# A hybrid DeltaNet / gMLP step: four weight pieces requested ahead of the second half of the modulation weights, and the halo rows in a tile of their own

## The chip, the cores and the metric

The kernel runs on one core of one Trainium2 chip. A core has five engines with a queue of instructions each: TensorE (PE, with the weight loads PEld), VectorE (DVE), ScalarE (ACT), GpSimd (POOL) and SyncE (SP), which here issues the DMA requests. The metric is the device time of one execution in microseconds. Before the change it was 2678.39 us, the median of three runs (2676.00 to 2682.14).

## The reference

One inference step of a layer over 128 context tokens and 2048 latent tokens, width 1024. Cut to what matters here:

```python
def modulation(cond, w_mod_l, b_mod_l):
    m = jax.nn.silu(cond) @ w_mod_l + b_mod_l
    return jnp.split(m[:, None, :], N_MOD, axis=-1)        # sh1, sc1, ga1, sh2, sc2, ga2

def mixer(h, s0, n_chunks, w_in_l, conv_l, ...):
    proj = h @ w_in_l
    qkv, gate, ab, u, vg = jnp.split(proj, cuts, axis=-1)
    qkv = jax.nn.silu(centred_conv(qkv, conv_l))           # width 3 over the tokens
    ...                                                    # bidirectional gated DeltaNet | gMLP
    return out @ w_out_l, s_new

def block(x, s0, mod, n_chunks, norm_mix_l, w_in_l, ...):
    sh1, sc1, ga1, sh2, sc2, ga2 = mod
    h = rmsnorm(x, norm_mix_l) * (1.0 + sc1) + sh1
    o, s_new = mixer(h, s0, n_chunks, w_in_l, ...)
    x = x + ga1 * o
    h = rmsnorm(x, norm_ffn_l) * (1.0 + sc2) + sh2
    x = x + ga2 * (jnp.square(jax.nn.relu(h @ w_ff1_l)) @ w_ff2_l)
    return x, s_new
```

`block` runs once for the context (modulated by the constant `c_ctx`) and once for the latent tokens (modulated by `c`). So the first projection `h @ w_in` needs the shift `sh1` and the scale `sc1` first, and those need `silu(cond) @ w_mod`.

## The kernel before

The 2176 tokens are 17 tiles of 128 rows. They are worked on in six blocks, five of three tiles and one of two. The kernel has three phases: the first projection with the convolution, the DeltaNet scan together with the gMLP and the output projection, and the feed-forward layer. The change lies at the start of the first phase.

Products of float32 are made in split form: an operand is cast to float32r on ScalarE (high part, `split_w`, line 194), and VectorE subtracts that from the original (low part, line 195). `mm3` (lines 220 to 222) then makes three matmuls of it: high by high, low by high, high by low.

At the start the shift and scale of the first norm are made by columns. The width of 1024 is eight column tiles of 128, and the vectors are made in halves of four column tiles. `mod_load(half, c0)` requests eight pieces of 128x512 of `w_mod`. `mod_columns` (from line 320) multiplies them with the two conditioning vectors in plain float32 (line 324), copies the resulting two rows on ScalarE (line 326), transposes them into columns (line 329) and adds the bias on VectorE (line 332); for the scale it adds one and multiplies by the norm's weight (line 336). There are four such calls: m0 gives the first half of the shift (`b1`), m1 the first half of the scale (`a1`), m2 and m3 the second halves of both.

The first block's rows (three tiles `x`, 512 KB each) are normalized by rows (`norm_rows`, line 301). The convolution looks one token to each side, so ten halo rows (`xh`) at the edges of the blocks are normalized, transposed and modulated apart (`hal`, `halH`, `halL`, `first_half`). Up to now `xh` takes one of the three buffers of the tag `x`, so that the third of the three row tiles waits until the halo rows have been transposed.

`column(k)` makes the operand of column tile k: three transposes on TensorE (line 471), scale and shift on ScalarE (`full`, line 473), then high and low part on VectorE (`kH`, line 476, and `kL`, line 477), plus single halo columns copied on GpSimd (lines 466 and 467). Columns 0 to 3 need the first halves of `a1` and `b1`, columns 4 to 7 the second halves. `feature_tile` then accumulates the eight columns against the pieces `W1` of `w_in`. The first three feature tiles of the first block are started by hand: columns 0 to 3 with their matmuls stand in the program ahead of `mod_columns(m2, ...)` and `mod_columns(m3, ...)`.

`make_masks` (from line 123) makes triangular masks for the scan: a memset on VectorE, twelve selects on GpSimd (lines 132 and 134), and differences on VectorE (lines 138 to 140).

The order on each engine is not the order of the program text. A planner goes through the instructions with its own estimate of the time and fixes, before anything runs, a sequence for each engine; on the chip each engine then keeps that sequence and waits on semaphores. SyncE issues the DMA requests in its sequence, with eight requests under way at a time: each waits for the landing of the one eight places ahead of it. Memory of a closed pool is used again by the pools of the next phase, whose first tiles wait for the last use of what lay there.

Of the kernel before, what the change touches and what calls it, by code (L numbers as in the profile page):

```python
# [8 lines left out]
F32 = mybir.dt.float32  # L9
# [8 lines left out]
P = 128  # L18
D = 1024
# [42 lines left out]
def hybrid_step(  # L62
# [118 lines left out]
    def raw_w(src, pool=None, tag="w"):  # L181
        t = (pool or wp).tile([P, 512], F32, tag=tag, name="raw")
        load(out=t, in_=src)
        return t
# [85 lines left out]
    with ExitStack() as ph:  # L270
        p1 = ph.enter_context(tc.tile_pool(name="p1", bufs=2, reuse_waits="tile"))
        pf = ph.enter_context(tc.tile_pool(name="p1f", bufs=2, reuse_waits="tile"))
# [43 lines left out]
        def mod_load(half, c0):  # L316
            return [raw_w(w_mod[0, k * P : (k + 1) * P, c0 + half * 512 : c0 + half * 512 + 512])
                    for k in range(KT)]

        def mod_columns(raws, half, dst, bias, scaled):  # L320

            pm = pm1()
            for k in range(KT):
                T.matmul(pm[0:2, :], scond[:, k, :], raws[k], start=k == 0, stop=k == KT - 1)
            row = p1.tile([2, 512], F32, tag="mrow", name="mrow", bufs=1)
            A.copy(row, pm[0:2, :])
            pc = pm1()
            for i in range(4):
                T.transpose(pc[:, 2 * i : 2 * i + 2], row[:, i * P : (i + 1) * P], ident[0:2, 0:2])
            ks = slice(half * 4, half * 4 + 4)  # L330
            d = dst[:, :, ks]
            V.tensor_tensor(out=d, in0=pc[:, 0:8].rearrange("p (k c) -> p c k", c=2),
                            in1=bias[:, ks].unsqueeze(1).to_broadcast([P, 2, 4]), op=ALU.add)
            if scaled:
                for cd in range(2):
                    V.scalar_tensor_tensor(out=dst[:, cd, ks], in0=dst[:, cd, ks], scalar=1.0,
                                           in1=vec[:, 16 + half * 4 : 20 + half * 4], op0=ALU.add, op1=ALU.mult)
# [25 lines left out]
        mod_columns(m0, 0, b1, vec[:, 0:8], False)  # L363


        xh = p1.tile([P, D], F32, tag="x", name="xh", bufs=3)[0:10, :]
        for m in range(5):
            r0 = 255 + 384 * m
            load(out=xh[2 * m : 2 * m + 2, :], in_=x_sample[0, r0 : r0 + 2, :])
# [9 lines left out]
        for t in BLOCKS[0]:  # L379
            x = p1.tile([P, D], F32, tag="x", name="x", bufs=3)  # L380
# [5 lines left out]
        def load_w1(gi, ks):  # L386
            return [w1_raw(gi, k) for k in ks]

        def w1_raw(gi, k):
            return raw_w(w_in[0, k * P : (k + 1) * P, gi * 512 : (gi + 1) * 512])  # L390
# [327 lines left out]
        blk, xs_, cols = prep_block(0)  # L718
        for st in xs_:
            st()  # L720
        m2 = mod_load(1, 0)
        m3 = mod_load(1, D)
        wr = load_w1(1, range(4))
        mod_columns(m1, 0, a1, vec[:, 8:16], True)
        W1[1] += [split_w(r) for r in wr]
        first_half(0)
# [3 lines left out]
        wr = load_w1(0, range(KT))  # L730
# [1202 lines left out]
```

## Time and profile before

| | us |
|---|---|
| median of three runs | 2678.39 (2676.00 to 2682.14) |
| the profiled execution: its time | 2678.03 |
| its span, first to last instruction | 2676.3 |
| TensorE busy | 2622.4 (98%) |
| VectorE busy | 1792.8 (67%) |
| ScalarE busy | 1245.4 (47%) |
| mean granted TensorE clock | 0.995 |

A row of a timeline gives the start, the duration, the engine, the line of the kernel, the operation, what it writes and reads, how many instructions are merged into the row, and in brackets the time that the engine stood idle before it and what ended that. A row of a view by stretches gives a stretch of time and the busy time of each engine in it, then the granted clock of TensorE (1.00 is full speed), the share of DMA that was busy, and GB/s. A matmul's duration is that of its passage through the array; back to back they start closer together than they last. A plain float32 matmul leaves two records.

### The profile page before, as it was taken

To read this page: it belongs to the slowest core of one execution; us is meant where nothing else is said; L and a number is where in the kernel's file an instruction comes from. 1 tells how busy PE (TensorE), PEld (TensorE's weight loads), DVE (VectorE), ACT (ScalarE), POOL (GpSimd) and SP (SyncE) were. 2 spreads that over 40 slices of the span, in tenths; PEclk is the share of its full clock that TensorE was granted. 3 is DMA by queue.
4 is the path that set the end of the run, shared out by engine and by line. 5 is a ranking of instruction groups with operands and counts; after the bars stand their busy time and mean duration, and the time that the engine had idled before them with its cause. 6 is when DMAs were issued, how large, how long until landed. Compare 5 with 4: busy or idle time off the path is not lost.

```text
span 2676.3 us, 45017 instructions
## 1 busy us (share of the span) xinstructions
PE 2622.4 (98%) x15698; PEld 2187.8 (82%) x15698; DVE 1792.8 (67%) x3694; ACT 1245.4 (47%) x3092; POOL 224.8 (8%) x448
## 2 busy tenths in 40 slices
PE   8999999999999999999999999999999999999998
PEld 5999998788887777788888888888888787888887
DVE  5867656766666778875688885566565556774874
ACT  4655555555554657763355543333242432332441
POOL 3111112111111111110000000000000000000000
PEclk9999999999999999999999999999999999999999
DMA  8867539655454657985868887443369978776772
GB/s 298 278 207 222 187 109 284 193 165 158 155 163 147 209 181 253 288 283 181 291 201 240 247 300 223 114 122 104 106 190 372 326 268 307 268 251 210 235 259 88
DMA packets 569385, 580.89 MB, mean 217 GB/s; under 512 B 35692, under 2 KB 401692, under 8 KB 565574
## 3 DMA queue, kind: packets, MB, share of 16 engines
q1 hardware_dynamic: 569158, 578.03, 67.6%
q8 instruction: 123, 2.02, 0.3%
q14 instruction: 104, 0.85, 0.1%
HBM read 398.14 MB, written 179.74 MB: 216 GB/s over the span
## 4 chain that ended last, share of the span: by engine, by line
PE 86%; DMA 6%; DVE 5%; ACT 1%; issue 1%; SPq 1%; POOL 0%; DVEq 0%; POOLq 0%; ACTq 0%
PE f L222 17%; PE f L220 17%; PE f L221 17%; PE pj L220 6%; PE pj L222 6%; PE pj L221 6%; PE pd L966 3%; PE pm L220 1%; PE pm L221 1%; PE pm L222 1%; PE pt L578 1%; PE pd L1140 1%; PE pd L1139 1%; DMA hop_d<-opL 1%; DMA qT<-qT_d 1%
## 5 line engine op out<-in xcount | busy, mean ns | idle before, releaser
L220 PE MATMUL f<-hop,zH 128*128 128x512 f32 x960 | 376.5, 393 | 1.2 <-ACT zH L1449 1.2
L221 PE MATMUL f<-hop,zH 128*128 128x512 f32 x960 | 377.1, 393 | 0.0
L222 PE MATMUL f<-hop,zL 128*128 128x512 f32 x960 | 376.9, 393 | 0.0
L220 PE MATMUL f<-hop,wH 128*128 128x512 f32 x896 | 354.0, 396 | 0.0
L221 PE MATMUL f<-hop,wH 128*128 128x512 f32 x896 | 350.7, 391 | 0.0
L222 PE MATMUL f<-hop,wL 128*128 128x512 f32 x896 | 350.6, 392 | 0.0
L1449 ACT CAST zH<-zraw 128x512 fp32r<-128x512 f32 x240 | 146.9, 621 | 297.1 <-DVE zraw L1443 86.4
L220 PEld LDWEIGHTS f<-hop,zH 128*128 128x128 f32 x960 | 180.4, 188 | 43.7 <-ACT zH L1449 1.6
L222 PEld LDWEIGHTS f<-hop,zL 128*128 128x128 f32 x960 | 180.3, 188 | 42.0 <-issue 0.9
L221 PEld LDWEIGHTS f<-hop,zH 128*128 128x128 f32 x960 | 180.1, 188 | 41.8 <-issue 0.9
L1443 DVE TENSOR_TENSOR zL<-zraw,zH 128x512 fp32r<-128x512 f32 x240 | 162.7, 687 | 66.4 <-ACT zH L1449 52.6
L222 PEld LDWEIGHTS f<-hop,wL 128*128 128x128 f32 x896 | 168.2, 188 | 37.6
L221 PEld LDWEIGHTS f<-hop,wH 128*128 128x128 f32 x896 | 168.5, 188 | 35.2
L220 PEld LDWEIGHTS f<-hop,wH 128*128 128x128 f32 x896 | 168.5, 188 | 34.8
L220 PE MATMUL pj<-kH,wH 128*128 128x386 f32 (+2 forms) x568 | 190.0, 337 | 0.3 <-DVE kH L476 0.3
L222 PE MATMUL pj<-kH,wL 128*128 128x386 f32 (+2 forms) x568 | 190.2, 335 | 0.0
L221 PE MATMUL pj<-kL,wH 128*128 128x386 f32 (+2 forms) x568 | 189.4, 334 | 0.0
L177 POOL TENSOR_TENSOR r<-rsq,nhalf 128x1 f32<-128x1 f32 (+1 forms) x38 | 23.4, 617 | 1480.2 <-DVE rsq L176 1480.2
L1443 DVE TENSOR_TENSOR wL<-raw,wH 128x512 fp32r<-128x512 f32 x112 | 76.1, 687 | 74.7 <-ACT wH L1449 73.7
L526 DVE SCALAR_TENSOR_TENSOR cv<-pj,vec,cv 128x384 f32<-128x384 f32 (+2 forms) x164 | 87.1, 538 | 55.1 <-ACT cv L523 53.8
L220 PEld LDWEIGHTS pj<-kH,wH 128*128 128x128 f32 x568 | 107.2, 189 | 4.8 <-issue 4.2
L1449 ACT CAST wH<-s 128x512 fp32r<-128x512 f32 x96 | 59.3, 620 | 108.6 <-DVE s L1443 108.3
(398 smaller groups left out, 6036.1 us busy)
## 6 DMA issues: line engine op xcount, KB each, us to landing
zraw<-z_d SPq DMA_DIRECT2D x212, 256.0 KB
raw<-in_w_ff_dram SPq DMA_DIRECT2D x128, 256.0 KB
hop<-hop_d SPq DMA_DIRECT2D x28, 1024.0 KB
z_d<-c SPq DMA_DIRECT2D x96, 256.0 KB
zraw<-s_d SPq DMA_DIRECT2D x96, 256.0 KB
raw<-in_w_mod_dram SPq DMA_DIRECT2D x80, 256.0 KB
r<-in_w_ff_dram SPq DMA_DIRECT2D x80, 256.0 KB
s_d<-s SPq DMA_DIRECT2D x64, 256.0 KB
```

The source lines that it names most:

```text
L177: G.tensor_tensor(out=out, in0=t[:np_, :n], in1=nhalf[:np_, :n], op=ALU.pow)
L220: T.matmul(ps, lh, rh, start=first and i == 0, stop=False, skip_group_check=more)
L221: T.matmul(ps, lh, rl, start=False, stop=False, skip_group_check=more)
L222: T.matmul(ps, ll, rh, start=False, stop=last and i == n - 1, skip_group_check=more)
L526: V.scalar_tensor_tensor(out=cv[:, o : o + m], in0=ps[:, s + sh : s + sh + m], scalar=convw[:, w, j : j + 1], in1=cv[:, o : o + m], op0=AL ...
L578: T.matmul(ps[:, i * P : (i + 1) * P], kTt[:, i * P : (i + 1) * P], rhs[:, i * P : (i + 1) * P], start=True, stop=True)
L966: T.matmul(p[:, h, :], lhs[:, h, :], rhs[:, h, :], start=True, stop=True)
L1139: T.matmul(p[:, h, :], u["qT"][:, h, :], s[:, h, :], start=True, stop=False)
L1140: T.matmul(p[:, h, :], u["QK"][:, h, :], u["vn"][:, h, :], start=s is None, stop=True)
L1443: V.tensor_tensor(out=out, in0=a, in1=b, op=op)
L1449: A.copy(h, src)
```

## The change

Two edits. The ten halo rows get a tile of their own, in the pool `pf` (`p1f`) in place of a buffer of the tag `x`, so that all three row tiles of the first block have a buffer from the start. And the first four pieces of `w_in` for the keys (`load_w1(1, range(4))`) are requested ahead of the sixteen pieces of `w_mod` for m2 and m3 in place of behind them.

```diff
@@ -363,7 +363,7 @@
         mod_columns(m0, 0, b1, vec[:, 0:8], False)
 
 
-        xh = p1.tile([P, D], F32, tag="x", name="xh", bufs=3)[0:10, :]
+        xh = pf.tile([P, D], F32, tag="xh", name="xh", bufs=1)[0:10, :]
         for m in range(5):
             r0 = 255 + 384 * m
             load(out=xh[2 * m : 2 * m + 2, :], in_=x_sample[0, r0 : r0 + 2, :])
@@ -718,9 +718,9 @@
         blk, xs_, cols = prep_block(0)
         for st in xs_:
             st()
+        wr = load_w1(1, range(4))
         m2 = mod_load(1, 0)
         m3 = mod_load(1, D)
-        wr = load_w1(1, range(4))
         mod_columns(m1, 0, a1, vec[:, 8:16], True)
         W1[1] += [split_w(r) for r in wr]
         first_half(0)
```

In the built program of the changed kernel TensorE's sequence after m1 is: m1's transposes, the third row tile's first transpose, then m2's eight products mixed with the matmuls of columns 0 to 3, m2's transposes, m3's eight products, twelve matmuls of a fourth feature tile, m3's transposes, ten matmuls for the modulation rows and the decay columns, and then columns 4 to 7. VectorE's sequence between m2's shift and m3's scale holds seven further low parts of `w_in` behind the first four, the memset of the masks and most mask differences. The requests on SyncE run: the ten halo rows, three row tiles, four pieces of `w_in`, sixteen of `w_mod`, then the rest.

## The prediction

> **What bounds the kernel now.** I read the page first, then the engines' busy time by stretches, then the timelines of TensorE, SyncE (the DMA requests), VectorE, ScalarE and GpSimd around the edit, which acts in the first 60 us.
>
> ```profile
> span 2676.3 us, 45017 instructions
> PE 2622.4 (98%) x15698; PEld 2187.8 (82%) x15698; DVE 1792.8 (67%) x3694; ACT 1245.4 (47%) x3092; POOL 224.8 (8%) x448
> ```
>
> TensorE is busy 2622.4 of 2676.3 us, so it idles 53.9 us in all. The edit removes no matmul; it can only move idle time or change the clock. The stretches say where idle time is:
>
> ```profile
> 0.00:20.00 20.00, 14.88 (x34) 2.98 (x35) 3.26 (x18) 4.70 (x8) 8.34 (x58) 1.00 0.83 287
> 20.00:40.00 20.00, 18.33 (x61) 4.88 (x58) 8.52 (x28) 7.52 (x15) 4.44 (x27) 1.00 1.05 378
> 40.00:60.00 20.00, 19.68 (x119) 19.31 (x119) 19.93 (x67) 13.48 (x30) 9.02 (x20) 1.00 0.67 227
> 60.00:120.00 60.00, 58.05 (x348) 54.63 (x347) 44.47 (x104) 43.85 (x135) 9.76 (x37) 1.00 0.86 280
> 120.00:440.00 320.00, 320.00 (x2024) 305.51 (x2023) 217.39 (x445) 173.90 (x539) 58.31 (x137) 1.00 0.63 196
> 440.00:520.00 80.00, 69.13 (x459) 52.91 (x458) 49.86 (x140) 40.80 (x105) 17.49 (x19) 0.92 0.79 242
> ```
>
> The columns are the length, then the busy time of TensorE, its weight loads, VectorE, ScalarE and GpSimd, the granted clock, the DMA share and GB/s. Between 20 and 40 us DMA is full (share 1.05) and TensorE idles 1.67 us; from 40 us TensorE is all but full. All that a perfect start could return after 20 us is 1.67 + 0.32 + 1.95 = 3.9 us, 0.15% of the time. That is the ceiling of the gain in this stage, and 0.2% (5.4 us) is about what a measurement of this kernel can tell from no change.
>
> The idle time between 20 and 41 us, gap by gap (start, duration, then in brackets the idle time before and what ended it):
>
> ```profile
> 22.68 0.33 PE L471 MATMUL pt<-ident,x 128*128 128x128 f32 x1 [0.48 <-DVE x L309]
> 23.28 7.03 PE L324 MATMUL pm<-raw,scond 128*2 128x512 f32 x16
> 31.03 0.41 PE L329 MATMUL pm<-ident,mrow 2*128 2x2 f32 x4 [0.72 <-ACT mrow L326]
> 31.36 7.03 PE L324 MATMUL pm<-raw,scond 128*2 128x512 f32 x16
> 39.11 0.41 PE L329 MATMUL pm<-ident,mrow 2*128 2x2 f32 x4 [0.46 <-ACT mrow L326]
> 40.49 0.59 PE L220 MATMUL pj<-kH,wH 128*128 128x388 f32 x2 [0.32 <-DVE kH L476]
> 41.93 0.34 PE L221 MATMUL pj<-kL,wH 128*128 128x388 f32 x1
> 42.11 0.34 PE L222 MATMUL pj<-kH,wL 128*128 128x388 f32 x1
> ```
>
> The two rows of 7.03 us are the second halves of the modulation vectors (m2, m3: eight products each, two records a product, so 0.88 us a product). The projection starts only behind both, and then a matmul starts every 0.18 us.
>
> **The change, part by part.** In the built program of the changed kernel the only moves are in the order of work; every engine keeps its instructions.
>
> (a) Requests. Today's order on SyncE (the first number is the time of the request):
>
> ```profile
> 14.96 0.35 SPq L381 DMA_DIRECT2D x<-in_x_sample_dram  x1
> 15.59 10.22 SPq L183 DMA_DIRECT2D raw<-in_w_mod_dram  x16
> 26.17 1.01 SPq L183 DMA_DIRECT2D raw<-in_w_in_dram  x2
> 27.60 0.33 SPq L381 DMA_DIRECT2D x<-in_x_sample_dram  x1
> 31.59 1.29 ACT L194 CAST wH<-raw 128x512 fp32r<-128x512 f32 x2 [0.62 <-DMA raw<-in_w_in_dram]
> ```
>
> Sixteen requests of 256 KB go out 0.66 us apart, and the weights requested at 26.17 are first used at 31.59: 5.4 us from request to use while the queue is full. In the changed order the third row tile (512 KB, so 1.3 us; with the halo rows in their own tile it need not wait for them) and four pieces of w_in (2.6 us) go ahead of m2. Its first piece is then requested at 15.59 + 1.3 + 2.6 = 19.5 and lands at 24.9. TensorE is ready for it at 23.3. **Cost +1.5 us** (0 if requests run at the pace of the emptier queue before 15 us, 2.5 if the 512 KB tile counts twice). The later 16 pieces arrive 0.66 us apart, TensorE needs 0.88 us each: no further wait. The third tile's square now stands ahead of m1's row copy on ScalarE and delays it by about 1.3 us, inside the same wait; all that is requested later keeps its place, since as many bytes are ahead of it.
>
> (b) Waits that go. The built order puts the 36 matmuls of the first four columns (36 x 0.18 = 6.4 us) around m2: 24 of them stand between m2's last product and its transposes, and twelve others behind m3's. They hide the two row copies and the first column's wait: 0.72 + 0.46 + 0.32 = **-1.5 us**. What was gained by starting early is thus just paid for by the late first piece. Moving the work itself gains nothing, TensorE was not idle while it did m2 and m3.
>
> (c) A new wait. The second half of the scale (a1) is needed by columns 4 to 7. On VectorE, which works in order, the built program puts ahead of it four low parts of w_in that follow the shift (b1), the memset for the masks, and the mask differences that need GpSimd's last mask. Today the masks are made far from the path:
>
> ```profile
> 36.78 1.28 DVE L195 TENSOR_TENSOR wL<-raw,wH 128x512 fp32r<-128x512 f32 x2
> 23.59 0.23 DVE L336 SCALAR_TENSOR_TENSOR a<-a,vec 128x4 f32<-128x4 f32 x2
> 23.86 0.88 DVE L396 TENSOR_SCALAR hal<-hal,a,b 128x10 f32<-128x10 f32 x4
> 42.98 0.22 DVE L476 CAST kH<-full 128x128 fp32r<-128x128 f32 x1
> 41.62 1.72 ACT L473 ACTIVATE full<-pt,b,a 128x128 f32<-128x128 f32 x4 [1.26 <-PE pt L471]
> 47.54 3.55 POOL L132 TENSOR_SCALAR_AFFINE_SELECT bd<-one 128x128 f16<-128x128 f16 x6 [3.76 <-DVE one L126]
> 51.05 3.48 POOL L134 TENSOR_SCALAR_AFFINE_SELECT bd<-bd 128x128 f16<-128x128 f16 x6
> ```
>
> Counted from the end of m2's transposes. VectorE: b1 0.2, four low parts 4 x 0.64 = 2.6, memset 0.1, GpSimd's twelve selects 7.0 (47.54 to 54.53), one difference 0.1, two low parts 1.3, three differences 0.4, the add and the two scalings 0.4: a1 is ready at 12.1. Then halo columns 0.9 and five casts and differences ahead of column 4's operand 1.3: its first matmul at 14.3 (ScalarE's three pieces, 3 x 0.43 = 1.3, run beside it). TensorE in the same time: m3 7.0, three transposes 0.25, twelve matmuls 2.1, four transposes 0.4, two matmuls of the modulation rows 0.4, eight of the decay columns 1.4: 11.6; six transposes (0.5) wait for ScalarE inside the gap. **Cost +2.2 us**, from 0 (masks done early) to 4 (weights late: the four low parts wait for pieces that land just then).
>
> (d) The clock. Two gaps of 2 to 3.5 us now hold almost no long matmul: 21.4 to 24.9 and about 51 to 54. What such gaps do today:
>
> ```profile
> 516.65 1.97 PE L966 MATMUL pd<-S,kT 128*128 128x128 f32 x8 [1.49 <-DMA S<-in_state_delta_dram]
> 516.00:518.00 2.00, 1.34 (x7) 1.38 (x8) 0.00 (x0) 1.95 (x6) 0.00 (x0) 0.68 1.05 307
> 518.00:520.00 2.00, 2.00 (x11) 1.38 (x11) 1.33 (x5) 0.10 (x1) 0.00 (x0) 0.50 0.18 53
> 829.65 0.28 PE L1048 MATMUL pd<-P,X 128*128 128x64 f16 x4 [2.01 <-DVE P L1040]
> 830.00:832.00 2.00, 2.00 (x11) 1.26 (x10) 0.86 (x2) 1.28 (x3) 0.00 (x0) 0.69 1.06 354
> 832.00:834.00 2.00, 2.00 (x19) 1.84 (x17) 0.89 (x2) 0.92 (x3) 0.00 (x0) 0.50 0.43 122
> 952.39 0.29 PE L1048 MATMUL pd<-P,X 128*128 128x64 f16 x4 [1.06 <-DVE P L1040]
> 952.00:954.00 2.00, 1.61 (x23) 1.51 (x24) 1.26 (x4) 1.11 (x5) 0.64 (x1) 1.00 0.74 172
> ```
>
> After gaps of 1.49 and 2.01 us the granted clock fell to 0.50; the lost shares of the two rows behind each, (0.32 + 0.50) x 2 and (0.31 + 0.50) x 2, are 1.6 us each. After a gap of 1.06 us it stayed at 1.00. Both new gaps are on the long side: **+1.6 us each, +3.2 us**; bounds 0 and 3.2. The Trainium skill (TensorE: Matmul & The Clock Gate, "Why this matters for your kernels") would have matmul bursts no more than about 3 us apart, and would let the 2.2 us of (c) pass at full speed. By that rule the sum below would be without the clock's term; the row at 829.65, a drop behind 2.01 us, speaks against it here.
>
> (e) Later. From 60 to 120 us two waits for split modulation weights cost 0.9 us:
>
> ```profile
> PE pm L348 <- ACT wH L194: 0.9, 2, 0.5
> ```
>
> TensorE comes some us later and DMA does not: I take back **0.5 us** (bounds -0.9 and, as the second such piece is now wanted soon after 54 us, +2). The halo tile shifts the second pool by 4 KB, so that the next phase's first tiles lie over other ones: the first decay tile now waits for the value stores that today hold up GpSimd.
>
> ```profile
> 450.44 0.64 POOL L994 TENSOR_SCALAR_AFFINE_SELECT Es<-E 128x512 f32<-128x512 f32 x1 [9.23 <-DMA vt_d<-tk]
> 457.40 0.64 POOL L1006 TENSOR_SCALAR_AFFINE_SELECT KK<-KK 128x512 f32<-128x512 f32 x1 [5.61 <-DMA hL<-hL_d]
> ```
>
> That makes this step some 1.9 us later, with 5.6 us of waiting behind it: zero, 1.9 if that cover were gone. Behind 520 us the order on TensorE is unchanged but for a few rows, and I put that at nothing.
>
> Sum: 1.5 - 1.5 + 2.2 + 3.2 - 0.5 = +4.9 us. The profiled execution took 2678.03 us (span 2676.3), the median of the runs is 2678.39: **2683 us**, a loss of 0.18%, at the edge of what can be told.
>
> **The rivals.**
> - *The clock holds.* Small transposes may count as activity, and gaps may be cut by the clock's own window. Then 2678.03 + 2.2 - 0.5 = 2679.7. For it: after the 0.72 us gap at 31.03 nothing happened. Against it: the rows above. The skill's rule gives this time too. 0.2.
> - *The other side: the masks do not hold a1.* GpSimd took 0.58 us for each 128x128 select while VectorE was full; a 128x512 select at 450.44 took 0.64. If selects run faster beside an idler VectorE, twelve in under 4.8 us, the wait of (c) is gone; with it the clock mostly holds: 2678.03 + 0 - 0.5 = 2677.5, no slower. 0.15; a few hundredths of it lie beyond -0.2%, if the 8 us lost at 460 to 470 also shrink.
> - *More is late.* The pieces of w_in that b1 queues ahead of, or the second modulation piece, land 2 to 3 us late, and each microsecond counts in full: 2683 + 3 = 2686, up to 2690 with one more drop of the clock in the next phase. 0.17.
>
> **How the numbers follow.** The forecast has the remaining 0.48. Its own spread (one clock drop or two, 1.6 us; executions of the kernel differ by 6 us) is 2680 to 2686, and about half of it lies above 2683.75. Slower by over 0.2%: 0.25 + 0.17 = 0.42; within: 0.23 + 0.2 + 0.09 = 0.52; faster: 0.06. The range runs from the second rival to the third: 2677 to 2689.
>
> **What would show it.** In the changed profile: m2's first product at 24.5 to 25.2 instead of 23.28 (a); no wait for the row copies of m2 and m3 (b); a wait of TensorE of 1.5 to 3 us near 54 us for column 4's operand, with GpSimd's selects between 42 and 50 us (c); the granted clock below 1.00 in 24 to 30 and 54 to 60 us (d). I am wrong if the masks are done early, if column 4 follows without a gap, or if the time moves where the order did not, behind 440 us.

## The result, and the profile after

| | before | changed |
|---|---|---|
| median, runs side by side (16 each) | 2682.51 us (2676.00 to 2691.65) | 2689.75 us (2686.92 to 2694.54) |
| ratio, 95% interval | | 1.0027 (1.0018 to 1.0035) |
| profiled execution | 2678.03 us | 2689.33 us |
| TensorE busy, idle, in the profile | 2622.4, 53.9 us | 2628.5, 59.1 us |

The change costs 0.27%, 7.2 us. The forecast was 2683 us, +4.9 us on the profiled execution. The time lies 0.75 us above the upper end of the range.

Two things differ between the medians and the profiles. The profiled execution of before was a quick one, 4.5 us below its median. And the executions of one kernel spread by 8 to 16 us, in part with the granted clock: over 35 runs of before that stood beside the first experiments, the mean span was 2683.8 us where the clock averaged 0.992 (3 runs), 2682.9 at 0.993 (12), 2679.6 at 0.994 (12), 2679.0 at 0.995 (7) and 2673.8 at 0.997 (1); at one and the same clock they still differed by up to 11 us. Span times clock estimates what an execution would take at the full clock. That gives 2668.7 us for the changed kernel (mean clock 0.9927) and 2664.1 us for before (0.9938): of the loss some 4.6 us are waits and order, some 3 us clock.

The engines' busy time by stretches of the changed kernel (length, then busy time of TensorE, its weight loads, VectorE, ScalarE, GpSimd, then clock, DMA share, GB/s):

```profile
20.00:40.00 20.00, 17.50 (x64) 6.77 (x63) 11.15 (x39) 9.46 (x21) 7.53 (x27) 0.91 1.02 361
40.00:60.00 20.00, 17.29 (x77) 9.93 (x76) 15.21 (x47) 11.27 (x23) 8.97 (x16) 1.00 0.67 222
60.00:120.00 60.00, 59.19 (x350) 56.86 (x350) 40.67 (x101) 40.49 (x125) 10.39 (x42) 1.00 0.79 252
120.00:160.00 40.00, 35.78 (x211) 34.32 (x209) 31.04 (x62) 21.96 (x71) 4.46 (x5) 0.96 0.65 206
440.00:520.00 80.00, 71.98 (x464) 56.72 (x463) 50.59 (x134) 45.17 (x120) 25.86 (x18) 0.89 0.82 251
...
24.00:26.00 2.00, 1.08 (x6) 0.59 (x7) 1.46 (x7) 0.29 (x2) 0.43 (x1) 0.76 1.05 397
26.00:28.00 2.00, 2.00 (x3) 0.25 (x2) 2.00 (x11) 2.00 (x5) 0.81 (x4) 0.50 1.06 394
28.00:30.00 2.00, 2.00 (x10) 1.05 (x9) 2.00 (x4) 0.76 (x2) 2.00 (x4) 0.88 1.06 387
```

Against the rows of before (in the prediction; from 120 to 440 us TensorE never idled there): idle time +0.8 us at 20 to 40, +2.4 at 40 to 60, -1.1 at 60 to 120 and +4.2 at 120 to 160 us; and the clock's loss, 0.09 x 20 = 1.8 us at 20 to 40 and 0.04 x 40 = 1.6 us at 120 to 160. Together 9.7 of the 11.3 us between the two profiles. From 440 to 520 us 2.9 us of idle time come back and the clock takes about 2 us more (0.89 for 0.92, both rounded); so 2 to 3 us are placed by none of these rows. The first 60 us cost 5.0 us, and the stretch from 120 to 160 us costs 5.8, which no step of the prediction had.

TensorE's waits in the changed kernel (start, duration, in brackets the idle time before and what ended it):

```profile
14.22 7.03 PE L324 MATMUL pm<-raw,scond 128*2 128x512 f32 x16
...
23.24 0.33 PE L471 MATMUL pt<-ident,x 128*128 128x128 f32 x1 [1.15 <-DVE x L309]
24.13 0.41 PE L329 MATMUL pm<-ident,mrow 2*128 2x2 f32 x4 [0.56 <-ACT mrow L326]
25.27 0.47 PE L471 MATMUL pt<-ident,x 128*128 128x128 f32 x1 [0.73 <-DVE x L309]
25.80 3.18 PE L324 MATMUL pm<-raw,scond 128*2 128x512 f32 x4
25.80 0.09 PEld L324 LDWEIGHTS pm<-raw,scond 128*2 128x2 f32 x2 [0.35 <-DMA raw<-in_w_mod_dram]
18.85 12.00 SPq L183 DMA_DIRECT2D raw<-in_w_mod_dram  x16
...
54.92 0.44 PE L598 MATMUL pm<-kH,abW 128*128 128x388 f32 x1 [0.61 <-DVE a L332]
57.29 1.01 PE L471 MATMUL pt<-ident,x 128*128 128x128 f32 x6 [0.68 <-ACT full L473]
59.70 0.62 PE L220 MATMUL pj<-kH,wH 128*128 128x388 f32 x2 [1.41 <-POOL kH L466]
...
129.02 0.44 PE L598 MATMUL pj<-kH,abW 128*128 128x386 f32 x1 [0.90 <-DVE cv L526]
132.97 0.55 PE L538 MATMUL pt<-ident,x 128*128 128x128 f32 x3 [0.50 <-ACT ev L581]
136.34 0.45 PE L220 MATMUL pj<-kH,wH 128*128 128x386 f32 x1 [2.82 <-DVE cv L526]
```

First group: m2 starts at 25.80 instead of 23.28 (the first row is m1's products, which end at 21.25). TensorE's last idle time before it is for VectorE's norm of the third row tile (line 309), whose transpose the planner has put ahead of m2. But that transpose ends at 25.74, and the weight load of m2's first product then still waits for its piece of `w_mod`, requested at 18.85 (the last two rows of the group). So the late piece sets m2's start. Second group: 2.7 us in three pieces. Third group: the new loss. VectorE and GpSimd behind these waits:

```profile
126.32 1.42 DVE L250 SCALAR_TENSOR_TENSOR acc<-raw,scond,acc 128x512 f32<-128x512 f32 x2 [2.59 <-DMA raw<-in_w_mod_dram]
...
119.71 0.96 SPq L235 DMA_DIRECT2D raw<-in_w_mod_dram  x2
...
57.35 2.81 POOL L466 CAST kH<-halH 128x1 fp32r<-128x1 f32 x4 [4.44 <-DVE halH L399]
...
57.35:60.10 2.75, 1.34 (x8) 0.96 (x9) 2.75 (x12) 2.28 (x6) 2.75 (x4) 1.00 0.47 149
```

```profile
113.09 0.59 SPq L235 DMA_DIRECT2D raw<-in_w_mod_dram  x1
```

At 126.32 VectorE waits 2.59 us for the second piece of `w_mod` that it sums up, which SyncE requested at 119.71, 6.6 us earlier. In before (the last row) that piece was requested at 113.09, and VectorE took it up 5.3 us later without a wait. So two things differ: VectorE comes to the sum 4.0 us after the request (126.32 - 2.59 - 119.71), and the piece takes at least 1.3 us longer. Behind the waiting instruction in VectorE's order stand the sums of the convolution (`cv`, line 526), for which TensorE waits 0.90 and then 2.82 us. GpSimd's row shows four copies of one halo column each (line 466): 2.81 us beside a VectorE that is busy all the time, 2.30 of them the first copy alone, and TensorE's 1.41 us at 59.70 end with them.

### The profile page after: what moved, and what is told of

It is laid out like the page before. It is cut to its first block, busy times and chain, and to the rows that moved or that the text cites. A ratio compares the mean times of both kernels' runs of the same rounds, so it can differ in the third digit from the quotient of the medians.

```text
span 2687.6 us, 45008 instructions
## 1 busy us (share of the span) xinstructions
PE 2628.5 (98%) x15698; PEld 2189.9 (81%) x15698; DVE 1791.3 (67%) x3694; ACT 1247.3 (46%) x3092; POOL 225.6 (8%) x448
## 4 chain that ended last, share of the span: by engine, by line
PE 85%; DMA 7%; DVE 4%; ACT 1%; issue 1%; SPq 1%; POOL 1%; DVEq 0%; POOLq 0%; ACTq 0%
PE f L222 17%; PE f L220 17%; PE f L221 17%; PE pj L220 6%; PE pj L221 6%; PE pj L222 6%; PE pd L966 3%; PE pm L220 1%; PE pm L222 1%; PE pm L221 1%; DMA raw<-in_w_mod_dram 1%; PE pd L1139 1%; PE pd L1140 1%; PE pt L578 1%; DMA raw<-in_w_in_dram 1%
## 5 line engine op out<-in xcount | busy, mean ns | idle before, releaser
L221 PEld LDWEIGHTS pj<-kL,wH 128*128 128x128 f32 x568 | 107.9, 190 | 2.6 <-issue 0.9
```

The lines of the kernel that those rows point to most:

```text
L221: T.matmul(ps, lh, rl, start=False, stop=False, skip_group_check=more)
```

## Experiments

Each was timed beside runs of the kernel before on the same chip. Times are given as the ratio to it with its 95% interval, and in us of 2682.

### Each edit alone

```diff
# halo tile alone (before, with)
-        xh = p1.tile([P, D], F32, tag="x", name="xh", bufs=3)[0:10, :]
+        xh = pf.tile([P, D], F32, tag="xh", name="xh", bufs=1)[0:10, :]
# weights ahead alone (before, with)
+        wr = load_w1(1, range(4))
         m2 = mod_load(1, 0)
         m3 = mod_load(1, D)
-        wr = load_w1(1, range(4))
```

> The kernel before with the halo rows in their own tile, weights requested where they were. Theory 1 (the loss is made of stalls that need both edits): the third row tile comes early, m2 starts within 1.3 us of 23.28, its gap stays under 1.5 us and the granted clock at 1.00; the masks stand behind a1, so no wait near 54 us; no wait for a modulation piece between 120 and 160 us. Time -2 to +1 us against before. Rival (the 4-KB shift of the second pool costs time in the next phase): +4 us or more, and the lag arises behind 440 us.

> The kernel before with the four weight pieces requested ahead of m2, halo rows where they were. Theory 1: the late first piece of m2 (+1 to +2.5 us), one drop of the clock (+1.6), the hidden row copies (-1.5), no wait for masks near 54 us since a1 stands ahead of them: +1 to +3 us. Rival (moving the requests carries the whole loss, by itself): +7 us with VectorE's wait for a modulation piece at 120 to 160 us.

Measured: halo tile alone 1.0009 (0.9998 to 1.0019), +2.4 us where theory 1 had at most +1; weights ahead alone 1.0008 (0.9998 to 1.0019), +2.1 us. Neither is a loss that can be told from none, and neither reaches the 7.2 us of both together. The halo tile (first three rows) did what theory 1 said in the first 60 us and then lost more than it expected; the last row is the weights':

```profile
20.00:40.00 20.00, 19.14 (x62) 5.46 (x61) 9.16 (x27) 7.93 (x14) 4.89 (x27) 1.00 0.98 350
60.00:120.00 60.00, 56.97 (x351) 55.22 (x350) 47.06 (x109) 43.84 (x135) 10.96 (x37) 1.00 0.86 277
120.00:160.00 40.00, 38.82 (x225) 35.73 (x224) 33.71 (x68) 22.74 (x69) 4.45 (x5) 1.00 0.74 242
```

```profile
60.00:120.00 60.00, 56.06 (x324) 54.18 (x324) 42.09 (x102) 41.26 (x129) 10.98 (x37) 0.94 0.81 263
```

With the halo tile TensorE idles only 0.86 us from 20 to 60 us (1.99 in before), but 3.0 and 1.2 us in the two stretches behind. The rival that the 4-KB shift of the second pool costs time falls: the profile's lag (how much later the same work runs than in before) was 1.9 us by the end of the first phase's sums (348 us) and stayed there. With the weights alone the sum fits the expectation but not its terms: m2 started at 23.68 without a gap, the waits for the row copies stayed, and the loss lies from 60 to 120 us (3.9 us idle, clock 0.94). In these profiles both edits, each all but harmless where it acts, are paid for behind it.

### The masks

```diff
         V.tensor_tensor(out=abW[:, :, 16:32], in0=abr, in1=f32(abW)[:, :, 0:16], op=ALU.subtract)
-        make_masks()
...
+                if bi == 0 and n == 3: side.append(make_masks)
                 if n == 1:
                     ab1, ab2 = ab_block(blk, bi)
```

Made in the changed kernel, in before, and in before with each edit alone:

> The changed kernel with the masks made inside the first block's loop, so that neither GpSimd's selects nor the differences stand ahead of a1's second half on VectorE. Theory 1 (the wait near 54 us is the masks'): the 2.7 us near 54 go. If the collision of the modulation accumulation with late transfers at 120 to 160 us (4.2 us of waits and about 1.6 us of clock) hangs on the lag, it shrinks too and the time is 0 to +2 us against before; if it hangs on the written order alone, +4.5. Rival (a1 waits for weights that land late, not for masks): the wait near 54 us stays and the time is +7.

> The kernel before with only the masks moved into the first block's loop. Theory 1 (the masks cost only where they stand ahead of a1's second half, which they do not in the kernel before): 0 +-2 us against before. Rival 2 (moving the masks is a gain by itself, whatever the two edits do, since their place there loads GpSimd and VectorE or sorts the work between 100 and 160 us worse): -5 us or more, and then the gain of the changed kernel with later masks says nothing on the two edits.

> Halo rows in their own tile and the masks later, weights requested as before. Theory 1: as the halo tile alone (+2.5 us), 0 to +3, since no mask stood ahead of a1 there either. Rival 2: 5 us or more below the halo tile alone.

> Weights ahead of m2 and the masks later, halo rows as before. Theory 1: as the weights ahead alone (+2 us), 0 to +4. Rival 2: 5 us or more below that. If all three kernels with later masks lie near 0, the loss of the changed kernel needs all of it: both edits and the masks where they are.

| | masks where they were | masks later |
|---|---|---|
| before | 1 | 0.9994 (0.9986 to 1.0003) |
| halo tile alone | 1.0009 (0.9998 to 1.0019) | 1.0023 (1.0013 to 1.0033) |
| weights ahead alone | 1.0008 (0.9998 to 1.0019) | 0.9989 (0.9978 to 0.9999) |
| both (the change) | 1.0027 (1.0018 to 1.0035) | 0.9991 (0.9981 to 1.0002) |

With later masks the changed kernel is 9.7 us quicker, at -2.4 us. In before the masks' place is worth 1.6 us and cannot be told from nothing, against rival 2; but with the weights ahead alone it is worth 5 us, as rival 2 had it, and with the halo tile alone it costs 3.8. Neither account covers the four. In the changed kernel theory 1 was half right on the stall near 54 us, and that is not where most of the gain lies:

```profile
58.35 0.62 PE L220 MATMUL pj<-kH,wH 128*128 128x388 f32 x2 [1.41 <-POOL kH L466]
...
120.00:160.00 40.00, 39.49 (x233) 35.72 (x232) 32.48 (x64) 22.56 (x72) 4.25 (x5) 1.00 0.75 236
```

The two waits of 0.61 and 0.68 us are gone, 1.3 us; the 1.41 us for GpSimd's copies stay. The loss at 24 to 30 us stays as well (clock 0.91 from 20 to 40 us). The larger part, 3.7 us of waits and the drop of the clock, is gone from 120 to 160 us, where nothing was edited: the planner sorted that stretch anew.

The halo tile with later masks missed its expectation by 3 us, at +6.2 us. What it lost is this:

```profile
56.45 0.45 PE L221 MATMUL pj<-kL,wH 128*128 128x388 f32 x1 [3.55 <-POOL kL L467]
...
46.39 9.88 POOL L466 CAST kH<-halH 128x1 fp32r<-128x1 f32 x4 [16.52 <-DVE halH L399]
...
48.23:56.20 7.97, 4.66 (x29) 4.26 (x27) 7.75 (x22) 5.71 (x13) 7.97 (x4) 1.00 0.73 229
```

TensorE waits 3.55 us for GpSimd's halo columns of columns 4 to 7. GpSimd took 9.88 us for four copies of 128x1 while VectorE was busy for 7.75 of 7.97 us, and 1.03 us for the four behind, where VectorE paused for 0.52 us. So the copies are a second thing that the order of VectorE decides, and moving the masks has no price of its own: what it is worth depends on the order that comes out.

### The place of the weights, and the copies

```diff
# weights between (the changed kernel, with)
-        wr = load_w1(1, range(4))
         m2 = mod_load(1, 0)
+        wr = load_w1(1, range(4))
         m3 = mod_load(1, D)
# copies on VectorE (the changed kernel, with)
-                    G.tensor_copy(kH[:, col : col + 1], f32(halH)[:, k, j : j + 1])
-                    G.tensor_copy(kL[:, col : col + 1], f32(halL)[:, k, j : j + 1])
+                    (V if bi == 0 else G).tensor_copy(kH[:, col : col + 1], f32(halH)[:, k, j : j + 1])
+                    (V if bi == 0 else G).tensor_copy(kL[:, col : col + 1], f32(halL)[:, k, j : j + 1])
```

Each alone, and then the weights between with later masks, without and with the copies moved:

> The changed kernel with the four weight pieces requested between the two second modulation pieces instead of ahead of both. Theory 1: m2 starts at 24 us or earlier, the gap stays under 2 us, the clock at 24 to 30 us at 1.00: 2.5 to 4 us less than the changed kernel, so +3 to +5 against before; the wait near 54 us (masks partly ahead of a1) stays at 1 to 2.7. Rival (the late first piece is not what costs; the third row tile's norm sets m2's start): m2 still starts at 25 to 26 us, the clock falls as in the changed kernel, +7.

> The changed kernel with the weights between the two modulation pieces and the masks later. Theory 1: no gap at 24 us and no drop of the clock there (as with the weights between), no masks ahead of a1: the 1.4 us for GpSimd's copies of the edge columns stay, and the wait at 120 to 160 us is small: -4 to 0 us against before, the fastest so far. Rival (what is saved at the start is given back at 120 to 160 us, where VectorE waits for modulation pieces): +3 us or more with waits of TensorE at 120 to 160 us of 2 us or more.

> The changed kernel with the first block's one-column copies of the halo on VectorE instead of GpSimd. Theory 1: the wait of 1.41 us at 59.70 for GpSimd's copies goes, the masks' wait of 1.3 stays, the stretch from 120 to 160 us may be sorted anew: +4 to +6 us against before if it is not, 0 to +2 if it is. Rival (with the copies gone the same wait is for a1, since the masks are what holds it): 2.7 us near 54 to 60 us stay, +7.

> The weights between the two modulation pieces, the masks later, and the one-column copies of the halo on VectorE. Theory 1: TensorE idles less than 0.5 us between 20 and 160 us, the clock stays at 1.00 there; with 4.4 us below before already without the last edit: -4 to -6 us. Rival (the first phase's order decides, and it is sorted anew): anywhere from -4 to +5 us, with one or two waits of 1 us or more between 60 and 160 us.

Weights between: 1.0028 (1.0018 to 1.0038), no quicker than the changed kernel, although the first group of waits went as theory 1 said:

```profile
20.00:40.00 20.00, 20.00 (x79) 7.77 (x78) 12.71 (x41) 9.94 (x21) 6.44 (x26) 1.00 1.03 359
40.00:60.00 20.00, 16.19 (x73) 11.55 (x72) 14.31 (x48) 12.38 (x24) 9.94 (x20) 0.94 0.87 282
120.00:160.00 40.00, 37.62 (x221) 34.69 (x221) 38.20 (x75) 18.84 (x56) 4.61 (x4) 1.00 0.75 227
56.00:60.00 4.00, 3.01 (x10) 2.92 (x11) 2.61 (x10) 3.79 (x8) 1.77 (x8) 0.68 0.93 298
...
56.99 0.66 PE L220 MATMUL pj<-kH,wH 128*128 128x388 f32 x2 [2.92 <-POOL kH L466]
```

TensorE does not idle from 20 to 40 us. It loses 3.8 us from 40 to 60 us instead, 2.92 of them to GpSimd's copies; the clock falls there (0.68), and 2.4 us of waits are left at 120 to 160 us. What is saved in front was lost behind.

With later masks on top it is the quickest kernel of this study: 0.9984 (0.9975 to 0.9992), 4.3 us less than before, 11.5 less than the changed kernel.

```profile
20.00:40.00 20.00, 20.00 (x78) 7.57 (x77) 12.24 (x39) 10.00 (x20) 6.49 (x26) 1.00 0.99 346
40.00:60.00 20.00, 19.19 (x97) 14.69 (x96) 13.68 (x38) 11.07 (x22) 2.96 (x8) 1.00 0.80 264
60.00:120.00 60.00, 59.81 (x368) 58.09 (x367) 47.55 (x118) 45.41 (x139) 17.34 (x49) 1.00 0.84 274
120.00:160.00 40.00, 39.88 (x230) 36.72 (x229) 34.40 (x67) 22.17 (x74) 5.09 (x5) 1.00 0.71 226
```

It idles 1.1 us between 20 and 160 us, where before has 3.9, and the clock stays at 1.00. The rival fell.

Copies on VectorE in the changed kernel: 1.0009 (1.0000 to 1.0018), +2.4 us. TensorE idles 0.55 us from 40 to 60 us instead of 2.7, so the rival falls, although 1.2 us of that come back as idle time from 60 to 120 us; the stretch from 120 to 160 us was sorted anew only in part:

```profile
120.00:160.00 40.00, 37.42 (x218) 35.73 (x218) 31.02 (x63) 22.37 (x70) 4.46 (x5) 0.96 0.68 227
...
133.32 0.41 PE L220 MATMUL pj<-kH,wH 128*128 128x386 f32 x1 [2.52 <-DVE cv L526]
```

On the quickest kernel the moved copies gave nothing more: 0.9988 (0.9979 to 0.9997), -3.2 us, 1 us to the other side and within the intervals. There the wait for them was 0.61 us.

### The stretch from 120 to 160 us

Whether it is the modulation sums' own doing or follows from the lag of the first 60 us was tried three ways. First all sums one tile later, then one step, each with a control in before:

```diff
-MOD_STEPS = (1, 1, 0, 0, 0, 1, 0, 2, 0, 1, 1, 2)
+MOD_STEPS = (1, 1, 0, 0, 0, 0, 1, 0, 2, 0, 1, 1)   # all later
+MOD_STEPS = (1, 1, 0, 0, 0, 0, 1, 2, 0, 1, 1, 3)   # one step later
```

> The changed kernel with the modulation sums of VectorE (from the fifth piece on) begun one tile later in the first block; the order up to 60 us is that of the changed kernel. Theory 1 (the loss of 120 to 160 us is the sums' pieces, requested when DMA is full, with the convolutions queued behind them on VectorE): the stretch's waits (4.2 us) and its drop of the clock (1.6 us) go, the first 60 us stay as in the changed kernel: 4 to 6 us less than that, +1 to +3 against before. Rival (the stretch is late because everything before it is, wherever the sums stand): waits of 3 us or more stay between 100 and 180 us, and the time is +6 to +8.

> The kernel before with the modulation sums begun one tile later, as a control. Theory 1: the stretch from 120 to 160 us has no wait to lose there: -1 to +2 us against before. Rival (later sums are a gain by themselves): -4 us or more.

> The changed kernel with the first step of the sums one tile later in the first block and as many steps in that block as before (so nothing moves in the later blocks). Theory 1 (the sums' pieces, requested while DMA is full, hold the convolutions on VectorE): the 4.2 us of waits and the drop of the clock between 120 and 160 us shrink to 2 us or less, no wait arises behind 160 us: 3 to 5 us less than the changed kernel, +2 to +4 against before. Rival (the lag from the first 60 us makes the stretch late wherever the sums stand): 3 us or more of waits stay there, +6 to +8.

> The kernel before with the same shift of one step, as a control: -2 to +2 us against before by both theories, without a wait behind 160 us. If it is 4 us or more to either side, the shift has an effect of its own and the run before it is read as a difference to this one.

Neither answered by its time. All later: 1.0055 (1.0043 to 1.0068) in the changed kernel and 1.0046 (1.0033 to 1.0059) in before. In the changed kernel the waits for the convolution's sums are gone from 120 to 160 us, 2.06 us are left (first row) and the clock stays at 1.00 there, as theory 1 has it. But both kernels lose 5 us near 333 us, again to GpSimd's copies:

```profile
132.71 0.55 PE L538 MATMUL pt<-ident,x 128*128 128x128 f32 x3 [2.06 <-ACT ev L581]
335.43 0.69 PE L221 MATMUL pj<-kL,wH 128*128 128x386 f32 x1 [4.22 <-POOL kL L467]
...
330.46 4.91 POOL L467 CAST kL<-halL 128x1 fp32r<-128x1 f32 x2
335.79 0.18 POOL L463 CAST kH<-zcol 128x1 fp32r<-128x1 f32 x1
...
330.46:335.30 4.84, 0.63 (x2) 0.30 (x2) 4.84 (x8) 0.52 (x1) 4.84 (x3) 0.70 1.00 332
```

```profile
332.34 1.01 PE L220 MATMUL pj<-kH,wH 128*128 128x386 f32 x2 [4.96 <-POOL kH L466]
```

One step later: 1.0048 (1.0031 to 1.0066) in the changed kernel, 1.0008 (0.9997 to 1.0020) in before. The stretch kept its waits (0.78, 0.50 and 2.82 us), since the sums stand where they stood: the planner takes up a piece as soon as its buffer is free, wherever the step stands in the program. A wait of 3.59 us for GpSimd's copies at 269 us came on top.

```profile
135.63 0.65 PE L220 MATMUL pj<-kH,wH 128*128 128x386 f32 x1 [2.82 <-DVE cv L526]
269.42 1.01 PE L220 MATMUL pj<-kH,wH 128*128 128x386 f32 x2 [3.59 <-POOL kH L466]
```

So the sums were tied to a value that is made only later, the first column of the third block. The steps of the sums move to later blocks with them, and `mod_steps` takes its factors from the argument `sc` (that part is left out here):

```diff
-MOD_STEPS = (1, 1, 0, 0, 0, 1, 0, 2, 0, 1, 1, 2)
+MOD_STEPS = (1, 1, 0, 0, 0, 1, 0, 2, 0, 1, 1, 1)
...
-        mods = [st for jc in range(4, 10) for st in (split_mod_steps(jc) if jc == 4 else mod_steps(jc, p1))]
+        mods = [st for jc in range(4, 10) for st in (split_mod_steps(jc) if jc == 4 else mod_steps(jc, p1, sc=scond2))]
...
-                nm = MOD_STEPS[n] if bi == 0 else n != 6
+                nm = MOD_STEPS[n] if bi == 0 else n != 6 if bi > 2 else 2 * (n not in (6, 7)) if bi == 2 else n >= 9
...
+                if bi == 1 and n == 8: side.insert(0, lambda kL=nxt[0][1]: V.scalar_tensor_tensor(out=scond2.rearrange("p k c -> p (k c)"), in0=f32(kL[0])[:, 1:17], scalar=0.0, in1=scond.rearrange("p k c -> p (k c)"), op0=ALU.mult, op1=ALU.add))
```

> The changed kernel with the modulation sums' factors copied by an instruction that also reads the first column of the third block, so that no sum can run before that; the order up to 60 us is that of the changed kernel. Theory 1 (the sums and their late pieces on VectorE make the waits of 120 to 160 us): no wait of TensorE over 1 us between 110 and 150 us and the clock at 1.00 there, although the lag from the first 60 us is all there. The time may still be that of the changed kernel, as the sums have to be done later; the lag at 150 us is what is read: 5 to 6 us instead of 11. Rival (the stretch is late because of the lag from the first 60 us): waits of 3 us or more stay between 110 and 150 us without any sum on VectorE.

> The kernel before with the same tie, as a control: by both theories no wait of TensorE over 1 us between 110 and 150 us. Behind 150 us the sums stand elsewhere in both, so the difference of these two is the price of the first 60 us alone: +4 to +7 us by theory 1, +8 to +12 by the rival.

Measured: 1.0006 (0.9997 to 1.0015) in the changed kernel, 0.9990 (0.9980 to 1.0000) in before; by the medians 2683.93 and 2678.55 us, 5.4 us apart (4.3 by the ratios).

```profile
55.39 0.45 PE L598 MATMUL pm<-kH,abW 128*128 128x388 f32 x1 [0.60 <-DVE a L332]
57.76 1.00 PE L471 MATMUL pt<-ident,x 128*128 128x128 f32 x6 [0.67 <-ACT full L473]
60.17 1.01 PE L220 MATMUL pj<-kH,wH 128*128 128x388 f32 x2 [1.41 <-POOL kH L466]
133.72 0.55 PE L538 MATMUL pt<-ident,x 128*128 128x128 f32 x3 [0.84 <-ACT ev L581]
...
60.00:64.00 4.00, 3.83 (x13) 3.74 (x14) 1.83 (x8) 0.94 (x3) 1.53 (x8) 0.59 0.65 212
120.00:160.00 40.00, 39.13 (x241) 37.65 (x240) 26.83 (x57) 22.84 (x78) 4.32 (x5) 1.00 0.65 201
```

The first 60 us are those of the changed kernel, with all their waits. From 120 to 160 us TensorE idles 0.87 us instead of 4.2, and the clock stays at 1.00. The rival falls: the lag alone does not make the stretch slow. Whether the changed kernel's order of sums would wait without the lag is not shown. The tied sums save the changed kernel 0.21%, 5.6 us, and before, which had no wait there, 0.10%, 2.7 us. So not all of the 5.6 us can be put to the stretch. The price of the first 60 us, 4.3 to 5.4 us, is the better settled part, though the interval of each ratio is about 2.5 us to either side. Only 2 to 3 us are left for the stretch in the net time, no more than these intervals, where its rows show 5.8 us in the one profile. How much of that the changed kernel would have got back later by itself stays open.

## Why the prediction was right and wrong

(a) and (b). The mechanism held, with other sizes. m2's first piece was requested at 18.85 (19.5 forecast) but served only just before 25.80 (24.9 forecast): 6.9 us from request to use, not 5.4. So m2 started 2.5 us later than in before, the upper bound of the term that the sum has at 1.5, and 0.6 us later than the latest time given. The third row tile's norm and transpose, which the working did not count ahead of m2, fit into that wait. The three waits of (b) are gone as forecast (no wait before m2's and m3's transposes). In idle time the two terms together cost 0.5 us, where the sum has nothing. With the weights between, and with the weights ahead alone, m2 started at 23.24 and 23.68 without a gap; so it takes the tile and the pieces together ahead of m2 to make it late.

(c) The wait came, 2.7 us for 2.2 forecast, but only half for the reason given. Masks and low parts ahead of `a1` account for 0.61 + 0.68 = 1.3 us, which went when the masks were moved. The other 1.41 us are GpSimd's four copies of halo columns. The working counted VectorE's halo columns and casts and left out the copies that follow them on GpSimd, although they are the last input of column 4.

(d) The first drop came: 0.76, 0.50 and 0.88 in the three rows from 24 to 30 us, (0.24 + 0.50 + 0.12) x 2 = 1.7 us for 1.6 forecast. The second did not: the clock stayed at 1.00 from 40 to 60 us, and in the two other profiles with the same order there as well. With the tied sums the same three waits (0.60, 0.67 and 1.41) were followed by 0.59 from 60 to 64 us, 1.6 us. So a gap cut into three by small matmuls decides nothing by its length here; one in four profiled executions lost the clock. The Trainium skill (TensorE: Matmul & The Clock Gate, "Why this matters for your kernels") keeps bursts within about 3 us of each other. By that rule, with every matmul counted, neither drop was due: at 24 us the trace differs from it, as it did in before behind 2.01 us, and near 60 us three of four traces agree. If the small transposes do not count, the long matmuls stand 4.5 us apart at 24 us (21.25 to 25.80), and that drop agrees with it too; no run here tells the two readings apart. The term's sum, 3.2 us, came out (about 3 us by the mean clock of the runs), but by luck: another drop came at 136 us.

(e) is the step that failed, "Later". It took back 0.5 us for 60 to 120 us and gave no term to 120 to 440 us, without a reason. From 60 to 120 us 1.1 us did come back. From 120 to 160 us waits of 4.2 us and the drop of 1.6 us came. The tied sums show that the lag alone does not make them: in the new order a sum stands on VectorE before its piece has landed, and the convolution's sums stand behind it. The prediction looked for what the two edits move and did not compare the order of the stretch behind them, where the planner had put other instructions next to each other.

The sum up to 60 us came out, +5.4 before (e) was taken off, against 5.0 in the rows and 4.3 to 5.4 between the kernels with tied sums. That is luck in part: the waits were 1.0 us above the forecast (3.2 for 2.2), the clock's loss 1.4 below it (1.8 for 3.2). The loss that was missed made 0.18% into 0.27%.

The base of the sum was too low as well. It was one execution at 2678.03 us, near the median of three runs, 2678.39; the 16 runs side by side have 2682.51. Of the 6.75 us between 2683 and 2689.75 that is 4.5, and the loss itself was only 2.3 us above the forecast. From 2682.51 us the same sum gives 2687.4, inside the range.

Of the rivals, the clock did not hold and the masks did hold `a1`. "More is late" gave the time that came (2686 to 2690, with one more drop of the clock), by a different mechanism: no piece that `b1` waits for was late, and the drop on top came at 136 us.

## What to carry to other kernels

Where a planner fixes the order, an edit of two lines is a new order for hundreds of microseconds behind it. Compare that order engine by engine beyond the edit, above all for instructions that wait for a transfer and have work of the critical path queued behind them. Take small copies on a slow engine into the chain, with what the other engines do meanwhile. And measure the order itself: four kernels in which only the place of the masks was changed moved by -10 to +4 us. Where executions spread by as much as the effect, take the base of a forecast from many of them.

## What was not expected of the hardware

GpSimd's copies of one column (128x1) last 0.18 us each from 335.79 us on, where VectorE is idle (with the sums later). Just before, from 330.46 to 335.30, two of them took 4.91 us with VectorE busy all the time; 9.88 us for four with the halo tile and later masks. It is single copies that are held up: one of these four lasted 7.81 us, and the two behind it 0.18 us each. GpSimd's spans are rough in these profiles, but TensorE's own waits of 1.41 to 4.96 us end with these copies. In before four of them took 1.15 us beside a VectorE just as busy, so it is not every stretch. The Trainium skill (SBUF — State Buffer, "Who interferes with whom") says that a VectorE instruction with two inputs from SBUF and a GpSimd instruction that reads SBUF exclude each other. The traces agree in kind (the low parts and sums on VectorE have two such inputs), but single copies waited through many VectorE instructions, of which none lasted over 1 us for one operation. That this exclusion is the cause is not shown by any run here.

The mean time falls with the mean granted clock by some 2 us for each 0.001 (2683.8 us at 0.992, 2673.8 at 0.997), which is a part of the spread between executions of one kernel: at 0.995 they still lie between 2674.9 and 2686.1 us.
